# One core, a mixture-of-experts stage: whole experts in order, with an expert's down products behind the next expert's gate and up products

## The chip, the cores and the metric

The kernel runs on one NeuronCore of a Trainium2 chip. The metric is the device time of one launch in microseconds: 894.48 is the median of three runs of the kernel before (893.54 to 895.44). A profile shows one further execution. The core has a matrix engine (PE, its weight loads on a row of their own, PEld), a vector engine (DVE), a scalar engine (ACT), a general engine (POOL) and a queue engine (SP); transfers are issued by SP, ACT and POOL and run on 16 DMA engines.

## The reference

One layer of a streaming encoder over 576 tokens (512 of a prompt, 64 of a sample), all float32: modulation, a normalised projection, two attention mixers, a merge, and then the part that matters here, a mixture of 32 experts:

```
combine = sum(one_hot(expert_id, 32) * w_top)          # two experts of one group per token
for e in range(N_EXPERTS):
    act = silu(n @ w_e_gate[e]) * (n @ w_e_up[e])      # (tokens, 1024) @ (1024, 256), twice
    out = out + combine[:, e] * (act @ w_e_down[e])    # (tokens, 256) @ (256, 1024)
y = y + gate2 * out
```

Each expert has three matrices of 1 MiB: gate, up and down.

## The kernel before

Until about 630 us of the profile the kernel computes everything ahead of the experts, and routes: every expert gets up to 64 slots of tokens. Tokens beyond that go to a loop of overflow blocks at the end, which runs as often as a count read from memory says.

**Rows of tokens.** The normalised rows lie in DRAM (`h2_d`, printed `h_d` by the profile). For two experts at a time `clear_rows` zeroes a tile `xg` of 128 rows on ACT, and `gather_rows` fills it by an indirect DMA on POOL's queue. `turned_rows` turns it into `xT` with 8 transposes on PE (tile `pxg`), and ACT and DVE each copy one half out. The tile `xg` has two buffers.

**One expert** is the generator `expert_parts`, which the program advances step by step: 8 steps of gate and up products into one PSUM tile `gu` (one step per 128 rows of the contraction; the gate product and the up product use two halves of the array), silu and the product `sl`, two small transposes `ta` and their copy `aT`, and the down products `dn`. DVE multiplies `dn` by the row gains `gw` and adds the result to `yr`, rows of the output that `take_rows` has gathered from DRAM. `put_rows` scatters `yr` back. Takes and puts are indirect DMAs on POOL's queue; the rows of an expert are taken two experts ahead.

**Order on PE** (lines 1816 to 1860): the down products of expert e stand inside the gate and up products of expert e+1: three steps of e+1, `ta` of e, two more steps of e+1, `dn` of e, then the last three steps of e+1. After the down products of every even expert stands `turned_rows` for the next two experts, and on POOL, behind the put of that expert, the gather for the two after those.

**Weights.** SP loads the matrices in a fixed order into a ring of 20 buffers (lines 1451 to 1490, `next_tile` counts with `turnstile`): gate, up, down of expert 0, then of expert 1, and so on. Before the first expert starts, 20 matrices have been asked for; from then on each load waits until the matrix that stood in its buffer is used up. At the end of the list the down matrix of expert 30 is held back until the up matrix of expert 31 is on its way (`load_next`). The order on each engine is the order in which the program records it (`manual_schedule`).

## Time and profile before

| | |
|---|---|
| median of three runs | 894.48 us |
| profiled execution, its own time | 895.09 us |
| its span | 893.1 us |
| PE busy | 796.2 us (89%) |
| POOL busy | 289.1 us (32%) |
| read from HBM | 186.86 MB |
| up matrices, from issue to landing | 21.6 us in the middle |
| put of rows, from issue to landing | 6.9 us in the middle |

The profiled execution's time is 2.0 us above its span, and 0.6 us above the median of the runs. In the views below a line names the program line, the engine, the operation and the tiles (out<-in); a figure in brackets is the idle time of the engine just before, and what ended it. [...] DMA share is the mean busy share of the 16 engines.

### The profile page before, as it was taken

How to read it: one execution, taken by the hardware profiler on the slowest of the kernel's cores; microseconds unless marked ns; L12 is line 12 of the kernel's file. 1: busy time of each engine (PE TensorE's matmuls, PEld its weight loads, DVE VectorE, ACT ScalarE, POOL GpSimd, SP SyncE). 2: the span in 40 equal slices, each digit the busy share in tenths (PEclk: the TensorE clock that was granted, in tenths of full speed). 3: DMA queues.
4: the chain of work that ended last, by engine and by line, in shares of the span. 5: the costliest groups of instructions: out<-in, count | busy, mean ns of one | idle time of the engine just before them, and what ended most of it. 6: DMA issues, size and time to landing. Idle time of an engine off the chain costs nothing.

```text
span 893.1 us, 16227 instructions
## 1 busy us (share of the span) xinstructions
PE 796.2 (89%) x6108; PEld 627.2 (70%) x6108; DVE 534.2 (60%) x1285; ACT 310.8 (35%) x754; POOL 289.1 (32%) x380
## 2 busy tenths in 40 slices
PE   6799999999899978999999999985799998878883
PEld 3567897877689967869999999984455554444441
DVE  3458999878956988647052445498355444342441
ACT  4363322475533546557232323432212212111210
POOL 1551432254447740412010103441233343332321
PEclk9899999999999989999999999996799999999997
DMA  9956778321012300126233129989699999999980
GB/s 307 344 168 217 263 242 297 104 62 61 17 61 88 108 4 2 49 97 172 71 95 95 49 97 345 350 301 405 186 415 414 413 412 407 415 413 401 416 333 36
DMA packets 78530, 194.95 MB, mean 218 GB/s; under 512 B 13587, under 2 KB 48387, under 8 KB 66419
## 3 DMA queue, kind: packets, MB, share of 16 engines
q1 hardware_dynamic: 68768, 174.85, 53.6%
q0 software_dynamic: 7424, 14.18, 4.7%
q10 hardware_dynamic: 2258, 4.87, 1.4%
q8 instruction: 49, 0.80, 0.4%
q14 instruction: 31, 0.25, 0.1%
HBM read 186.86 MB, written 18.01 MB: 229 GB/s over the span
## 4 chain that ended last, share of the span: by engine, by line
PE 46%; DMA 24%; DVE 18%; issue 5%; ACT 3%; POOL 2%; SPq 1%; POOLq 0%; DVEq 0%; ACTq 0%
DMA weu<-in_w_e_up 11%; DMA yr<-out_y,sidx 4%; PE pg L410 4%; PE pg L412 4%; PE pg L411 4%; PE gu L1602 3%; PE pj L215 3%; PE pj L217 3%; PE pj L216 3%; DVE K L904 2%; DVE acc L683 2%; DVE m L682 2%; DMA xg<-h_d,gidx 2%; DMA weg<-in_w_e_gate 2%; PE o L799 2%
## 5 line engine op out<-in xcount | busy, mean ns | idle before, releaser
L1602 PE MATMUL gu<-weu,xT 128*64 128x256 f32 x512 | 133.4, 402 | 21.7 <-DMA weu<-in_w_e_up 21.7
L1602 PE MATMUL gu<-weg,xT 128*64 128x256 f32 x512 | 132.2, 398 | 0.5 <-ACT sl L1606 0.5
L215 PE MATMUL pj<-whi,hT 128*128 128x256 f32 (+1 forms) x352 | 107.3, 305 | 0.9 <-DVE yn L472 0.6
L217 PE MATMUL pj<-whi,hT 128*128 128x256 f32 (+1 forms) x352 | 100.7, 286 | 1.3 <-DVE hT L234 1.3
L216 PE MATMUL pj<-wlo,hT 128*128 128x256 f32 (+1 forms) x352 | 100.5, 286 | 0.0
L1602 PEld LDWEIGHTS gu<-weg,xT 128*64 128x64 f32 x512 | 66.6, 141 | 40.8 <-issue 13.3
L203 DVE TENSOR_TENSOR wlo<-raw,whi 128x512 fp32r<-128x512 f32 (+1 forms) x72 | 53.5, 764 | 68.4 <-ACT whi L202 67.8
L1602 PEld LDWEIGHTS gu<-weu,xT 128*64 128x64 f32 x512 | 67.8, 142 | 33.7 <-DMA weu<-in_w_e_up 27.6
L1621 DVE TENSOR_TENSOR gw<-gw,dn 128x512 f32<-128x512 f32 x32 | 22.0, 688 | 105.6 <-PE dn L1619 105.6
L1643 POOL DMA_INDIRECT out_y<-yr,sidx x32 | 33.7, 1053 | 148.2 <-DVE yr L1622 139.2
L410 PE MATMUL pg<-hT,whi 128*128 128x256 f32 (+1 forms) x256 | 78.3, 306 | 0.0
L412 PE MATMUL pg<-hT,whi 128*128 128x256 f32 (+1 forms) x256 | 75.7, 296 | 0.0
L411 PE MATMUL pg<-hT,wlo 128*128 128x256 f32 (+1 forms) x256 | 75.7, 296 | 0.0
L215 PEld LDWEIGHTS pj<-whi,hT 128*128 128x128 f32 x352 | 67.1, 190 | 8.1 <-issue 4.9
L217 PEld LDWEIGHTS pj<-whi,hT 128*128 128x128 f32 x352 | 66.6, 189 | 1.6 <-DVE hT L234 1.5
L216 PEld LDWEIGHTS pj<-wlo,hT 128*128 128x128 f32 x352 | 66.9, 190 | 0.1
L203 POOL TENSOR_TENSOR wlo<-raw,whi 128x512 fp32r<-128x512 f32 (+1 forms) x32 | 41.9, 1332 | 74.2 <-ACT whi L202 54.4
L202 ACT CAST whi<-raw 128x512 fp32r<-128x512 f32 (+1 forms) x104 | 60.3, 624 | 14.8 <-PE pu L1134 14.8
L1619 PE MATMUL dn<-wed,aT 128*64 128x512 f32 x256 | 60.5, 594 | 0.8 <-ACT aT L1614 0.8
L410 PEld LDWEIGHTS pg<-hT,whi 128*128 128x128 f32 x256 | 48.5, 189 | 4.6 <-issue 4.3
L906 POOL TENSOR_TENSOR B<-B,K 128x512 f32<-128x512 f32 (+4 forms) x36 | 35.5, 985 | 41.5 <-DVE K L904 29.2
L411 PEld LDWEIGHTS pg<-hT,wlo 128*128 128x128 f32 x256 | 48.5, 190 | 0.2
(392 smaller groups left out, 2026.4 us busy)
## 6 DMA issues: line engine op xcount, KB each, us to landing
weg<-in_w_e_gate SPq DMA_DIRECT2D x26, 1024.0 KB, 16.5
weu<-in_w_e_up SPq DMA_DIRECT2D x26, 1024.0 KB, 21.6
wed<-in_w_e_down SPq DMA_DIRECT2D x26, 1024.0 KB, 18.5
raw<-in_w_in SPq DMA_DIRECT2D x20, 1024.0 KB, 5.6
wa<-in_w_ada SPq DMA_DIRECT2D x16, 512.0 KB, 10.6
va<-in_w_ada SPq DMA_DIRECT2D x8, 1024.0 KB, 5.3
obT<-in_w_ada SPq DMA_DIRECT2D x8, 1024.0 KB, 6.7
weg<-in_w_e_gate SPq DMA_DIRECT2D x12, 512.0 KB, 11.1
```

The costliest lines, as they stand in the source:

```text
L202: act.copy(hi[:, a:a + 2], raw[:, a:a + 2])
L203: eng.tensor_tensor(lo[:, a:a + 2], raw[:, a:a + 2], hi[:, a:a + 2].bitcast(F32), op=ALU.subtract)
L215: pe.matmul(p[:, :n], a, hi[:, k, :], start=(k == 0), stop=False)
L216: pe.matmul(p[:, :n], a, lo[:, k, :], start=False, stop=False)
L217: pe.matmul(p[:, :n], b, hi[:, k, :], start=False, stop=(k == KD - 1))
L410: pe.matmul(p[:, :b - a], hi[:, k, cs], hT[:, k, a:b], start=(k == 0), stop=False)
L411: pe.matmul(p[:, :b - a], lo[:, k, cs], hT[:, k, a:b], start=False, stop=False)
L412: pe.matmul(p[:, :b - a], hi[:, k, cs], hT[:, k, LP + a:LP + b], start=False, stop=(k == KD - 1))
L906: pool.tensor_tensor(B[:, :nk], B[:, :nk], K[:, 1:nk + 1], op=ALU.mult)
L1602: pe.matmul(gu[64 * j:64 * j + 64, 0:FE], xT[:, k], w[j][k // 4][:, k % 4, :], start=(k == 0), stop=(k == KD - 1))
L1619: pe.matmul(dn[64 * j:64 * j + 64, :], aT[:, k, :], w[2][k][:, 0, j * 512:(j + 1) * 512], start=(k == 0), stop=(k == 1))
L1643: ordered(pool.indirect_dma_start(out=y_rows, out_offset=bass.IndirectOffsetOnAxis(ap=idx_ap, axis=0), in_=yr, in_offset=None, bounds_chec ...
```

## The change

Whole experts follow one another on PE. The generator is split into `expert_up`, `expert_turn` and `expert_down`, and the loop reads: gate and up products of e, after an odd e the turned rows of the next two experts, the down products of e-1, the transposes of e. The list of loads is put in the order of use (`sequence`), and the special case at its end goes. The gather for the experts after next is issued in the iteration of an odd e, behind the put of expert e-1.

```diff
+    sequence = [(0, 0), (0, 1)]
+    for e in range(1, NE):
+        sequence += [(e, 0), (e, 1), (e - 1, 2)]
+    sequence.append((NE - 1, 2))
...
     def next_tile():
-        e, i = divmod(turnstile[0], 3)
+        e, i = sequence[turnstile[0]]
...
+        def down(e):
+            expert_down(aTs.pop(e), ahead.pop(e), gws.pop(e), yrs[e])
+            put_rows(yrs.pop(e), sidx[:, e:e + 1], e)
+
+        gain_rows(0)
+        for e in range(NE):
             j = 64 * (e % 2)
...
-        for e in range(1, NE):
-            begin(e, KD + 1 - 3 - 2)
-            begin(e + 1, 3)
-            begin(e, 1)
-            begin(e + 1, 2 if e < NE - 2 else KD + 1 - 3)
-            begin(e, 9)
-            put_rows(yrs[e], sidx[:, e:e + 1], e)
-            load_next(e)
...
-            if e % 2 == 0:
-                nxt.append(turned_rows(xg, 128))
+            sl = expert_up(xT[:, :, j:j + 64], ahead[e])
+            if e % 2 and e < NE - 1:
+                xT = turned_rows(xg, 128)
                 m = e // 2 + 2
                 if m < NE // 2:
                     xg = clear_rows()
-                    gather_rows(xg, gidx[:, m:m + 1], 128)
-            rows_ahead(e + 2)
+            if e:
+                down(e - 1)
+            gain_rows(e + 1)
+            aTs[e] = expert_turn(sl)
+            for _ in range(2 if e == 0 else 3):
+                if turnstile[0] < len(sequence):
+                    load_tiles(1)
+            if e % 2 and e < NE - 1 and m < NE // 2:
+                gather_rows(xg, gidx[:, m:m + 1], 128)
+            if e + 2 < NE:
+                yrs[e + 2] = take_rows(sidx[:, e + 2:e + 3], e + 2)
...
+        down(NE - 1)
```

On PE, around the turned rows (`pxg`) of experts 4 and 5, it stood like this before; `gu` are products with gate (`weg`) and up (`weu`) matrices, `dn` down products, `ta` the small transposes:

```order
L1612 MATMUL ta<-ident,sl 128x64 x2
L1602 MATMUL gu<-weg,xT 64x256
L1602 MATMUL gu<-weu,xT 64x256
L1602 MATMUL gu<-weg,xT 64x256
L1602 MATMUL gu<-weu,xT 64x256
L1619 MATMUL dn<-wed,aT 64x512 x4
L1582 MATMUL pxg<-ident,xg 128x128 x8
L1602 MATMUL gu<-weg,xT 64x256
```

And it stands like this now:

```order
L1606 MATMUL gu<-weg,xT 64x256
L1606 MATMUL gu<-weu,xT 64x256
L1587 MATMUL pxg<-ident,xg 128x128 x8
L1626 MATMUL dn<-wed,aT 64x512 x4
L1617 MATMUL ta<-ident,sl 128x64 x2
L1606 MATMUL gu<-weg,xT 64x256
```

The turned rows have moved from behind the down products of an even expert to between the last gate and up products of an odd expert and the down products of the expert before it.

On POOL's queue, at the first experts, it stood like this before; `yr` are rows taken, `out_y` rows put, `xg` the gathered rows of two experts, and the numbers tell the tiles apart (7695, 7699, ... belong to experts 0, 1, ...):

```order
L1573 DMA xg_7690<-h2_d_78,gidx_6535 128x1024
L1637 DMA yr_7695<-out_y,sidx_6533 128x512
L1637 DMA yr_7699<-out_y,sidx_6533 128x512
L1643 DMA out_y<-yr_7695,sidx_6533 1152x512
L1573 DMA xg_7763<-h2_d_78,gidx_6535 128x1024
L1637 DMA yr_7768<-out_y,sidx_6533 128x512
L1643 DMA out_y<-yr_7699,sidx_6533 1152x512
```

And now:

```order
L1578 DMA xg_7690<-h2_d_78,gidx_6535 128x1024
L1644 DMA yr_7695<-out_y,sidx_6533 128x512
L1644 DMA yr_7699<-out_y,sidx_6533 128x512
L1644 DMA yr_7740<-out_y,sidx_6533 128x512
L1650 DMA out_y<-yr_7695,sidx_6533 1152x512
L1578 DMA xg_7777<-h2_d_78,gidx_6535 128x1024
L1644 DMA yr_7805<-out_y,sidx_6533 128x512
```

The gather of experts 4 and 5 still stands behind the put of expert 0, but that put now comes after the turned rows of experts 2 and 3 and the gate and up products of expert 1; a third take stands ahead of it.

## Rows read from the trace of the kernel before

**Rows 1.** Windows: start:end, length, busy us of each engine, PEclk, DMA share, GB/s.
```profile
660.00:745.00 85.00, 81.03 (x588) 44.46 (x586) 42.38 (x70) 17.26 (x38) 34.76 (x32) 1.00 1.02 413
745.00:860.00 115.00, 93.89 (x588) 47.66 (x584) 42.56 (x71) 17.50 (x38) 35.66 (x32) 0.94 1.02 411
```
**Rows 2.** Waits of SP's queue, 700 to 860 us: total, times, longest.
```profile
SPq L1488 <- DMA weu<-in_w_e_up: 46.1, 21, 3.4
...
SPq L1488 <- PE gu L1602: 0.4, 2, 0.2
```
**Rows 3.** Timeline of PE: start, duration, line, tiles, [idle before].
```profile
775.42 0.43 PE L1602 MATMUL gu<-weu,xT 128*64 128x256 f32 x1 [1.78 <-DMA weu<-in_w_e_up]
...
820.26 0.43 PE L1602 MATMUL gu<-weu,xT 128*64 128x256 f32 x1 [3.13 <-DMA weu<-in_w_e_up]
...
870.89 0.43 PE L1602 MATMUL gu<-weu,xT 128*64 128x256 f32 x1 [1.02 <-DMA weu<-in_w_e_up]
```
**Rows 4.** Windows of 5 us from the end of each long wait of PE.
```profile
748.90:753.90 5.00, 4.99 (x24) 2.51 (x26) 0.00 (x0) 0.27 (x1) 0.00 (x0) 0.66 1.04 410
775.40:780.40 5.00, 4.98 (x24) 2.53 (x26) 0.00 (x0) 0.27 (x1) 0.26 (x1) 0.66 1.02 415
802.20:807.20 5.00, 4.99 (x32) 2.57 (x33) 0.32 (x1) 0.27 (x1) 0.00 (x0) 1.00 1.02 413
820.30:825.30 5.00, 5.00 (x24) 2.44 (x26) 0.00 (x0) 0.27 (x1) 0.00 (x0) 0.66 1.01 388
838.30:843.30 5.00, 5.00 (x26) 2.55 (x28) 0.00 (x0) 0.27 (x1) 0.00 (x0) 0.72 1.04 417
856.00:861.00 5.00, 4.96 (x32) 2.54 (x33) 0.29 (x1) 0.27 (x1) 0.09 (x1) 1.00 1.03 416
```
**Rows 5.** Chain of waits, 633 to 658 us: start, us, engine or transfer, tile.
```profile
633.68 8.61 DMA xg<-h_d,gidx
...
649.79 1.72 PE dn L1619 x8
651.50 2.59 PE gu L1602 x24
654.09 0.38 PE ta L1612 x2
...
657.20 1.02 PE pxg L1582 x8
```
**Rows 6.** Timeline, the end of expert 0's gate and up products.
```profile
638.10 0.33 SPq L1488 DMA_DIRECT2D wed<-in_w_e_down  x1
...
639.04 0.45 PE L1612 MATMUL ta<-ident,sl 64*128 64x64 f32 x2 [0.96 <-DVE sl L1607]
```
**Rows 7.** Timeline, from down products to a put, and from a put to a gather.
```profile
715.87 1.89 PE L1619 MATMUL dn<-wed,aT 128*64 128x512 f32 x8
...
719.49 1.10 POOL L1643 DMA_INDIRECT out_y<-yr,sidx  x1 [2.45 <-DVE yr L1622]
...
726.33 1.02 POOL L1643 DMA_INDIRECT out_y<-yr,sidx  x1 [4.17 <-PE gu L1602]
727.65 1.02 POOL L1573 DMA_INDIRECT xg<-h_d,gidx  x1 [0.31 <-issue]
```
**Rows 8.** Tile xg: its 16 gathers from issue to landing.
```profile
DMA to landing us min/median/max: 6.0/9.0/9.8
```
**Rows 9.** Timeline, the last two experts.
```profile
874.93 1.89 PE L1619 MATMUL dn<-wed,aT 128*64 128x512 f32 x8
...
876.75 0.45 PE L1612 MATMUL ta<-ident,sl 64*128 64x64 f32 x2
...
877.60 1.94 PE L1619 MATMUL dn<-wed,aT 128*64 128x512 f32 x8 [0.41 <-ACT aT L1614]
...
881.28 1.01 POOL L1643 DMA_INDIRECT out_y<-yr,sidx  x1 [1.71 <-DVE yr L1622]
```

## Prediction

> **What bounds the kernel now.** I read the busy time in windows first, then the waits of SP's queue, the waits of PE, and last the chain of waits through the first experts. From 660 to 860 us the DMA engines show a share of 1.02 at 411 to 413 GB/s without a break, so the weights stream at full rate [rows 1]. PE behaves in two ways under that stream. Up to 745 us it is busy 81.0 of 85 us: it works through the 20 matrices that lie ready at the start, and is itself the slower one. From 745 on it is busy 93.9 of 115 us: it has caught up and waits for the next up matrix [rows 1]. Six of those waits last 1.78 to 3.13 us; the shortest and the longest are shown [rows 3]. SP is not held up by PE: from 700 to 860 us its 21 waits on the landing of up matrices sum to 46.1 us, and its waits on gate and up products to 0.4 us [rows 2]. So buffers are free long before they are needed, and the end is set by the landing of the up matrix of expert 31, at 870.89 us [rows 3]. What follows is a fixed tail of down products, put and closing work.

> Two experts take about 17.8 us of the stream (waits end at 820.3, 838.3 and 856.0, two experts apart [rows 4]). PE needs about 12.3 us for them, as worked out below. The spare 5.5 us is what the change can use up before it costs anything.

> **The weights.** The first 20 loads of the new list are again experts 0 to 5 and the gate and up matrices of expert 6. The next two wait for the gate and up products of expert 0, whose end releases a load at 638.10 now [rows 6]; nothing ahead of that point moves. The last four loads are again gate 31, up 31, down 30, down 31, since the old list already held back down 30. The same bytes in the same ring therefore bring up 31 at the same time; I keep 870.89. This holds while PE gives back buffers faster than the stream fills them, that is below 17.8 us for two experts.

> **The tail.** Now it takes 877.60 - 870.89 = 6.71 us from up 31 to the start of the last down products [rows 3, 9]. After the change the transposes of expert 30 stand before that point. What is left is 16 pairs of products at 2.59 / 12 us each, 3.45, and 0.05 to start; the down products of expert 30, 1.72; and from the last transposes to the last down products 877.60 - 876.75 = 0.85 [rows 5, 9]. That is 6.07, a gain of 0.6 us. The work behind it, put and close, is the same. If PE comes late to that point, the delay is added whole.

> **The gathered rows.** This is the term that decides. In the new order the transposes `pxg` of an odd expert e stand ahead of the down products of e-1, those stand ahead of the put of e-1, the put ahead of the next gather on POOL, and that gather is what `pxg` of e+2 waits for. So there is a loop, once per two experts: `pxg` 1.02 [rows 5], from the start of the down products to the put 719.49 - 715.87 = 3.62, from the put to the gather behind it 727.65 - 726.33 = 1.32 [rows 7], the gather itself 9.0 in the middle [rows 8], and 0.04 to start PE: 15.0 us. PE's own work in the same stretch is two times (3.50 + 1.72 + 0.38) plus 1.02 = 12.2 [rows 5]. So PE would wait some 2.7 us at every `pxg`, 14 times (e = 3 to 29). In the old order the gather had the whole 12.2 us of PE's work between the put and the transposes, and hardly showed. A loop of this kind does not stand in the trace of before, so the gather's landing bounds it: at 6.0 the loop is 12.0 and PE's own work rules; at 9.8 it is 15.8. I take the middle, 9.0, to which nearly all of the 16 gathers lie close.

> When does the loop cost time? Expert 1 can start after the transposes of expert 0, at 639.04 + 0.37 = 639.41 [rows 6], and its products end at 642.9. The gather for experts 2 and 3 has landed at 642.29 [rows 5], so the first `pxg` starts at 642.9. From the last one, at e = 29, PE needs 1.02 + 1.72 + 0.38 + 3.50 + 1.72 + 0.38 = 8.7 us until it is ready for expert 31, so it must start by 870.89 - 8.7 = 862.2. Fourteen rounds may thus take 219.3 us, or 15.66 each. At 15.0 they end at 852.9, and 9.3 us are to spare.

> **The clock.** Those waits have a price of their own. [...] One fall costs (1 - 0.66) x 5 = 1.7 us, or 1.4; over all six waits that is 6.5 / 6 = 1.08 per wait. In the new order the wait ends at `pxg`, and what runs slowly first is `pxg` and the down products, 2.74 us of work that lies inside the loop. So nearly all of the loss lengthens the round, and the next wait is as long as this one. I take 1.0 per round. The bounds are 0 (no fall after waits of 2.7 us) and 1.7 (a fall every time). Fourteen rounds lose 14.0 us: the last `pxg` starts at 852.9 + 14.0 = 866.9, which is 4.7 us late.

> [...]

> **What is hidden.** Row gains for the next expert move on DVE behind the add of e-1; DVE is busy 42.4 of 85 us and has room [rows 1]. The takes now come three experts ahead of their use instead of two, so no add should wait for them. The third take ahead of the first put falls in the pause of the stream before 641 us.

> **Sum.** Tail -0.6, lateness +4.7, together +4.1 us: 899.2 for the profiled execution (895.09), which lies 0.6 above the median of the runs. For the median, 894.48 + 4.1 = 898.6.

> **Rivals.**
> First, the weights still set the end, and it is not slower. If the waits at `pxg` are followed by a lower clock in fewer than 5 or 6 rounds (9.3 us to spare, 1.7 each), or gathers land at 8.5 instead of 9.0 (7 us in 14 rounds), PE is ready when up 31 lands. For it: the gathers late in the trace are no slower than the early ones, and two of six waits cost nothing [rows 4, 8]. The time is 894.48 - 0.6 = 893.9. [...]

> Second, the lower clock follows every wait. Fourteen times 1.6, the mean of the four falls, is 22.4 us: `pxg` of e = 29 at 875.3, 13.1 late, and the time is 894.48 + 13.1 - 0.6 = 907.0. Against it stand the waits before 802.2 and 856.0, which left the clock at 1.00 [rows 4]. [...]

> Third, faster. Up 31 would have to land at least 1.2 us earlier and PE be ready for it. With equal bytes, equal start and an equal end of the list I see only the spread of the stream for it: about 892.

> **How the numbers follow.** The forecast, lateness from 0 to 11 us with its middle at 4.7, gets 0.54; the first rival 0.33; the second 0.08; the third 0.05. Within 0.2% (1.8 us, about what a measurement of this kernel can tell from no change) lie the first rival, except a little of it below, and the part of the forecast with less than 2.4 us of lateness (0.05): 0.37. Slower takes the rest of the forecast and the second rival: 0.57. Faster 0.06. The range goes from 893.2, just under the first rival's time, to 906.5, just under the second's; the forecast's own range is 894.5 to 905.

> **What the profile would show.** Right: PE's waits sit at `pxg` with the gather as releaser, some 14 of 2 to 3 us, starting at e = 3 near 655 us; the time between two `pxg` is about 16 us from 643 to 867; the granted clock falls after most of them; waits on up matrices nearly vanish, and expert 31 starts after 870.9. SP still waits on landings, not on PE, and the DMA share stays at 1.02 to about 860. Wrong: `pxg` finds its rows landed (gathers under 7 us, or a round of 12.5 us); or rounds of 15.5 and less with expert 31 waiting for its up matrix, which is the first rival; or SP waiting on PE, which would break the argument on the stream; or up 31 landing at another time than 869 to 872.

## The result, and the profile after

The changed kernel takes 907.43 us (median of 4 runs, 907.08 to 910.94); the kernel before takes 894.96 beside it (4 runs, 893.54 to 896.62). The ratio is 1.0139, with an interval from 1.0115 to 1.0163: slower by 12.5 us, where 4.1 were forecast and the range ended at 906.5. The profiled execution has a span of 905.8 us and a time of 907.68.

Busy time in windows of the changed kernel, the two that answer to [rows 1] (PE, PEld, DVE, ACT and POOL with instructions, then the granted clock as a share of full speed, the share of the DMA engines, GB/s):

```profile
660.00:745.00 85.00, 72.21 (x477) 37.85 (x477) 34.57 (x56) 15.58 (x32) 26.65 (x25) 0.92 1.01 409
745.00:860.00 115.00, 96.32 (x638) 51.74 (x640) 47.39 (x77) 19.65 (x42) 37.32 (x35) 0.91 1.02 413
```

The transfers are as busy as before, with shares of 1.01 and 1.02. PE is not: in the first window, where it was the slower one and worked at a granted clock of 1.00, it now runs 477 matmuls in 72.2 us at a clock of 0.92 and waits the rest of the time. The waits of PE from 640 to 880 us, and those of SP's queue from 700 to 860, which answer to [rows 2]:

```profile
PE pxg L1587 <- DMA xg<-h_d,gidx: 35.8, 14, 3.4
```

```profile
SPq L1493 <- DMA weu<-in_w_e_up: 41.6, 19, 3.4
SPq L1493 <- DMA wed<-in_w_e_down: 38.7, 19, 3.1
SPq L1493 <- DMA weg<-in_w_e_gate: 38.3, 19, 3.4
...
SPq L1493 <- PE gu L1606: 2.3, 4, 1.6
```

PE's waits on up matrices [rows 3] are gone. In their place stand 14 waits for gathered rows, 35.8 us in sum, all at `pxg`. SP still waits for landings, 118.6 us in the three lines; all its waits on work of PE sum to 3.6 us. The first and the third round of the loop in the timeline, the first at a granted clock of 1.00, the third behind a fall, at 0.50 from 677.10 to 682.10 us (start, us, engine, line, operation, tile; in brackets the wait before it):

```profile
645.13 1.09 PE L1587 MATMUL pxg<-ident,xg 128*128 128x128 f32 x8
...
649.83 1.14 POOL L1650 DMA_INDIRECT out_y<-yr,sidx  x1 [9.31 <-DVE yr L1629]
651.28 1.04 POOL L1578 DMA_INDIRECT xg<-h_d,gidx  x1 [0.31 <-issue]
...
660.97 1.09 PE L1587 MATMUL pxg<-ident,xg 128*128 128x128 f32 x8 [3.20 <-DMA xg<-h_d,gidx]
...
677.06 1.97 PE L1587 MATMUL pxg<-ident,xg 128*128 128x128 f32 x8 [3.44 <-DMA xg<-h_d,gidx]
678.95 3.68 PE L1626 MATMUL dn<-wed,aT 128*64 128x512 f32 x8
...
684.38 1.13 POOL L1650 DMA_INDIRECT out_y<-yr,sidx  x1 [10.48 <-DVE yr L1629]
685.82 1.03 POOL L1578 DMA_INDIRECT xg<-h_d,gidx  x1 [0.31 <-issue]
```

From `pxg` to the put it is 649.83 - 645.13 = 4.70 us at 1.00 and 684.38 - 677.06 = 7.32 behind the fall; from the put to the gather 1.45 (1.32 in [rows 7]); from the gather to the next `pxg` 660.97 - 651.28 = 9.69 here, 8.17 to 9.94 in the 14 rounds with a mean of 9.06. The gathers themselves, which answer to [rows 8], are as before:

```profile
DMA to landing us min/median/max: 5.0/8.9/9.9
```

The last two `pxg`, the down products of expert 28 behind the second, and the last rows, which answer to [rows 9]:

```profile
857.34 1.97 PE L1587 MATMUL pxg<-ident,xg 128*128 128x128 f32 x8 [2.80 <-DMA xg<-h_d,gidx]
...
873.55 1.37 PE L1587 MATMUL pxg<-ident,xg 128*128 128x128 f32 x8 [2.05 <-DMA xg<-h_d,gidx]
874.85 3.30 PE L1626 MATMUL dn<-wed,aT 128*64 128x512 f32 x8
...
890.34 1.94 PE L1626 MATMUL dn<-wed,aT 128*64 128x512 f32 x8 [0.41 <-ACT aT L1619]
```

Fourteen rounds take 873.55 - 645.13 = 228.4 us, 16.32 each, and the last down products start at 890.34 instead of 877.60, 12.7 us later: all of the loss stands before that point. Windows of 5 us behind a `pxg`, as in [rows 4] but with PE's columns alone (PE busy, granted clock, DMA share, GB/s):

```profile
661.00:666.00 5.00, 5.00 (x34) 1.00 1.02 414
677.10:682.10 5.00, 5.00 (x16) 0.50 1.03 415
...
709.40:714.40 5.00, 5.00 (x20) 0.66 1.00 380
740.40:745.40 5.00, 5.00 (x20) 0.66 1.03 421
...
873.60:878.60 5.00, 5.00 (x20) 0.66 0.08 30
```

Behind 10 of the 14 waits the clock is lower, 0.50 to 0.68 over the 5 us, and behind the other four it is 1.00; five of the windows are shown, the last one from the `pxg` of e = 29 on. The wait's length does not tell which: 3.20 us before 660.97 left the clock alone, 1.88 before 709.37 did not.

The start, which answers to [rows 5, 6] (DVE, ACT's queue, ACT, PE and SP's queue, by time):

```profile
628.25 0.19 DVE L1527 TENSOR_TENSOR wslot<-tbw,wslot 128x32 f32<-128x32 f32 x1
...
628.47 0.49 DVE L1598 TENSOR_SCALAR gw<-gate,wslot 128x512 f32<-128x512 f32 x1
...
632.83 0.33 ACTq L1569 DMA_DIRECT2D ov_d<-ovi  x1
...
633.76 0.58 ACT L90 COPY xT<-pxg 128x512 f32<-128x512 f32 x1 [9.20 <-DVE xT L92]
...
634.40 0.69 PE L1606 MATMUL gu<-weg,xT 128*64 128x256 f32 x1 [1.80 <-ACT xT L90]
...
640.21 0.33 SPq L1493 DMA_DIRECT2D weg<-in_w_e_gate  x1
```

The row gains of expert 0 (`gw`, two products of which the first is shown) now run on DVE inside the overflow chain, whose two small stores (`ov_d` and one more) stand on ACT's queue ahead of the evacuation of the first rows. The first release of a buffer is at 640.21, and was at 638.10.

### The profile page after: what moved, and what is told of

Read it like the earlier page. It is cut to its first block, busy times and chain, and to the rows that moved or that the text cites. A ratio compares the mean times of both kernels' runs of the same rounds, so it can differ in the third digit from the quotient of the medians.

```text
span 905.8 us, 16239 instructions
## 1 busy us (share of the span) xinstructions
PE 799.8 (88%) x6108; PEld 630.6 (70%) x6108; DVE 534.6 (59%) x1285; ACT 310.9 (34%) x754; POOL 287.0 (32%) x380
## 4 chain that ended last, share of the span: by engine, by line
PE 38%; issue 21%; DVE 18%; DMA 12%; POOL 6%; ACT 2%; SPq 1%; POOLq 0%; DVEq 0%; ACTq 0%
PE pg L410 4%; DMA out_y<-yr,sidx 4%; PE pg L412 4%; PE pg L411 4%; PE pj L215 3%; POOL yr L1644 3%; PE pj L217 3%; PE pj L216 3%; DVE K L904 2%; DVE acc L683 2%; DVE m L682 2%; POOL out_y L1650 2%; PE o L799 2%; DMA bc<-mod_d 2%; DVE wlo L203 1%
## 5 line engine op out<-in xcount | busy, mean ns | idle before, releaser
L1606 PE MATMUL gu<-weg,xT 128*64 128x256 f32 x512 | 119.5, 387 | 1.8 <-ACT xT L90 1.8
L1606 PE MATMUL gu<-weu,xT 128*64 128x256 f32 x512 | 119.5, 388 | 0.0
L1606 PEld LDWEIGHTS gu<-weg,xT 128*64 128x64 f32 x512 | 68.5, 139 | 37.9 <-ACT xT L90 2.2
L1650 POOL DMA_INDIRECT out_y<-yr,sidx x32 | 36.1, 1129 | 155.9 <-DVE yr L1629 155.9
L1626 PE MATMUL dn<-wed,aT 128*64 128x512 f32 x256 | 74.1, 709 | 0.4 <-ACT aT L1619 0.4
L202 ACT CAST whi<-raw 128x512 fp32r<-128x512 f32 (+1 forms) x104 | 60.3, 624 | 15.3 <-PE pu L1134 14.8
L1587 PE MATMUL pxg<-ident,xg 128*128 128x128 f32 x128 | 22.6, 334 | 38.2 <-DMA xg<-h_d,gidx 38.2
L1610 DVE TENSOR_TENSOR sl<-sl,gu 64x256 f32<-64x256 f32 x32 | 13.6, 424 | 61.2 <-ACT sl L1609 61.2
```

What stands on the lines that cost most here:

```text
L202: act.copy(hi[:, a:a + 2], raw[:, a:a + 2])
L1606: pe.matmul(gu[64 * j:64 * j + 64, 0:FE], xT[:, k], w[j][k // 4][:, k % 4, :], start=(k == 0), stop=(k == KD - 1))
L1626: pe.matmul(dn[64 * j:64 * j + 64, :], aT[:, k, :], w[2][k][:, 0, j * 512:(j + 1) * 512], start=(k == 0), stop=(k == 1))
L1650: ordered(pool.indirect_dma_start(out=y_rows, out_offset=bass.IndirectOffsetOnAxis(ap=idx_ap, axis=0), in_=yr, in_offset=None, bounds_chec ...
```

## The experiments

Each is timed beside the kernel before on the same chip, so the ratios are to be compared; the times of the kernel before differ by up to 2 us between the groups (894.96 to 896.98). Where an expectation says 2.4 or 1.2 GHz it means a granted clock of 1.00 or 0.50: the profile gives the clock as a share of full speed, and no run here shows a rate in GHz.

**The gather ahead of the put.** The loop of the new order is cut in one place:

```diff
                 if m < NE // 2:
                     xg = clear_rows()
+                    gather_rows(xg, gidx[:, m:m + 1], 128)
             if e:
                 down(e - 1)
...
-            if e % 2 and e < NE - 1 and m < NE // 2:
-                gather_rows(xg, gidx[:, m:m + 1], 128)
```

> The order of PE and of the loads stays as in the changed kernel; only the gather for the next two experts is issued earlier, straight behind the clearing of its tile, ahead of the down products of e-1 and of their put on POOL. Theory (the loop through put and gather sets the time): with the put out of the loop a round needs transposes 1.0, evacuation and clearing about 1.5, gather 9.1, some 11.6 us, less than PE's own 12.2 us. The 14 waits at the transposes, 35.8 us in the changed kernel, fall under 8 us in sum, the weights set the end again, and the last down products start near 879 instead of 890.3: 895 to 897 us. Rival (the new order of PE's work or the lower clock by itself sets the time): the rounds stay near 16.3 us and the time stays at 904 to 908. Second rival (the gather is now late behind the clearing): waits of about 1 us stay, and about 900 us.

Measured: 896.4 us, ratio 1.0003 (0.9994 to 1.0012): the whole loss is gone. Its waits of PE, 640 to 880 us, a window as in [rows 1], and a round in its timeline:

```profile
PE gu L1606 <- DMA weu<-in_w_e_up: 20.6, 11, 2.9
...
PE pxg L1587 <- DMA xg<-h_d,gidx: 0.7, 1, 0.7
```

```profile
745.00:860.00 115.00, 93.73 (x582) 49.52 (x583) 42.76 (x70) 17.06 (x37) 34.09 (x32) 0.91 1.02 411
```

```profile
657.22 1.09 PE L1587 MATMUL pxg<-ident,xg 128*128 128x128 f32 x8
...
660.58 1.00 POOL L1578 DMA_INDIRECT xg<-h_d,gidx  x1 [0.30 <-issue]
661.92 1.14 POOL L1650 DMA_INDIRECT out_y<-yr,sidx  x1 [0.35 <-issue]
...
669.94 1.09 PE L1587 MATMUL pxg<-ident,xg 128*128 128x128 f32 x8
```

The gather goes out 3.4 us after `pxg` instead of 6.15, ahead of the put, and a round is 669.94 - 657.22 = 12.7 us, PE's own work. The order of PE's work and that of the loads are those of the changed kernel, so the place of the gather behind the put is a necessary part of the loss. The lower clock alone is not enough for it: from 745 to 860 us PE is granted 0.91 here as in the changed kernel, with its waits now on weights, and nothing is lost.

**Work in the wait, 24 pairs.** In the changed kernel, products that nobody reads go into a spare PSUM bank ahead of each `pxg`; each writes with the weights of the expert just done:

```diff
+    def spin(n, w, xT=None):
+        f = mm_ps("spin")
+        for k in range(n):
+            for j in range(2):
+                pe.matmul(f[64 * j:64 * j + 64, 0:FE], ident[:, 0:64] if xT is None else xT[:, k % KD],
+                          w[j][k % KD // 4][:, k % 4, :], start=(k == 0), stop=(k == n - 1))
...
             if e % 2 and e < NE - 1:
+                spin(12, ahead[e], xT[:, :, j:j + 64])
                 xT = turned_rows(xg, 128)
```

> Changed kernel with 12 more pairs of gate and up products of the odd expert ahead of the transposes, into a spare PSUM bank that nobody reads: 2.6 us of PE work at full clock, placed where PE waits for the gathered rows. Theory (the wait itself costs little beyond the loop; the lower clock behind it lengthens 9 of 14 rounds by 1.7 us): PE keeps 2.4 GHz, every round takes 1.0 + 3.7 + 1.45 + 9.1 = 15.2 us, the transposes at e = 29 start near 858 instead of 873.6, expert 31 waits for its up matrix again, and the time falls to 896 to 898 us although PE has 36 us more to do. Rival (the clock falls for another reason than PE's pause, or the loop alone decides): rounds of 16.3 us or longer and 907 us or more.

Measured: 933.07 us, ratio 1.0418 (1.0403 to 1.0433). The time expected was missed because the edit was twice as large as I had meant: a written product is two instructions in the trace, and the filler takes 5.18 us. Windows of it, with the columns of [rows 1]:

```profile
660.00:745.00 85.00, 85.00 (x680) 50.22 (x678) 32.66 (x54) 13.48 (x29) 24.36 (x23) 1.00 1.01 404
745.00:860.00 115.00, 115.00 (x912) 67.38 (x910) 44.27 (x73) 17.89 (x39) 36.46 (x35) 1.00 1.01 402
```

PE is the bound, with rounds of 17.75 us, and in them it never pauses (85.00 of 85 us and 115.00 of 115) and its clock is 1.00. That is half of the answer.

**Work in the wait, 12 pairs.** The same, half as long.

```diff
             if e % 2 and e < NE - 1:
+                spin(6, ahead[e], xT[:, :, j:j + 64])
                 xT = turned_rows(xg, 128)
```

> As the run with products in the wait, but half as many: each written product is two instructions, so 12 written pairs were 24 pairs and 5.18 us, and PE itself became the bound (rounds of 17.75 us = 12.57 + 5.18, clock 1.00). Now 12 pairs, 2.59 us, so that PE's own round is 12.57 + 2.59 = 15.16 and the loop with gather 15.2. Theory (the lower clock behind the waits is a size of its own): clock 1.00, rounds of 15.2 to 15.5, transposes of e = 29 at 858 to 862, the weights set the end again: 896 to 898 us. Rival (the loop alone is 16.3 us long, whatever the clock): 906 to 908 us, with the waits only shorter by what the products take.

Measured: 895.9 us, ratio 0.9997 (0.9986 to 1.0007). PE has 15 times 2.59 = 39 us more to do than in the changed kernel and yet, by the two ratios (1.0139 and 0.9997), the kernel is 12.7 us faster. Its windows, its waits, a round, and the start of expert 31:

```profile
660.00:745.00 85.00, 83.71 (x640) 47.75 (x638) 36.71 (x60) 16.26 (x34) 27.85 (x27) 1.00 1.02 414
745.00:860.00 115.00, 113.27 (x868) 64.69 (x866) 51.38 (x84) 20.38 (x44) 41.65 (x39) 1.00 1.02 410
```

```profile
PE pxg L1587 <- DMA xg<-h_d,gidx: 3.0, 6, 0.9
```

```profile
756.19 1.09 PE L1587 MATMUL pxg<-ident,xg 128*128 128x128 f32 x8 [0.75 <-DMA xg<-h_d,gidx]
...
760.90 1.14 POOL L1657 DMA_INDIRECT out_y<-yr,sidx  x1 [7.82 <-DVE yr L1636]
762.35 1.03 POOL L1578 DMA_INDIRECT xg<-h_d,gidx  x1 [0.31 <-issue]
...
872.45 0.43 PE L1606 MATMUL gu<-weg,xT 128*64 128x256 f32 x1
```

The loop is still there: `pxg` to put 4.71, put to gather 1.45, and the gather behind it, 15.2 to 16.2 us a round. What is missing is the lower clock (1.00 in both windows, 0.92 and 0.91 in the changed kernel), and with it the loss. So loop and clock are needed together. Part of the expectation was missed: the weights do not set the end here. PE waits for no weight from 640 to 885 us; it starts expert 31 at 872.45, and the last update of the semaphore of up 31 in the trace is at 872.26. PE and the stream arrive level, and a round much longer would have shown in the time.

**Row gains of expert 0 behind the first takes.**

```diff
         yrs = {e: take_rows(sidx[:, e:e + 1], e) for e in range(2)}
+        gw0 = row_gains(wslot[:, 0, 0:1], wslot[:, 1, 0:1])
...
-        gws, aTs = {}, {}
+        gws, aTs = {0: gw0}, {}
-        gain_rows(0)
```

> Changed kernel with one edit: the two products of the row gains of expert 0 are written behind the first takes, in the block before, so that DVE runs them behind the overflow chain again. Theory (they held up ovi, the two small stores on ACT's queue, and behind these the evacuation of the first rows): the gate and up products of expert 0 start at 632.5 instead of 634.4, the first transposes of the loop at 643.1 instead of 645.1, and all that hangs on them, 1.9 to 2.2 us earlier: 905.3 us, since the loop has no slack. Rival (the start is late for another reason, or the loop takes the gain back): expert 0 starts at 634.4, or the time stays at 907.4.

Measured: 908.64 us, ratio 1.0141 (1.0127 to 1.0156): no gain. My theory of the start fell, as far as the time goes. The timeline of its profiled execution:

```profile
626.32 1.48 SPq L1493 DMA_DIRECT2D wed<-in_w_e_down  x2
...
631.14 0.33 ACTq L1569 DMA_DIRECT2D ov_d<-ovi  x1
...
635.70 1.97 PE L1587 MATMUL pxg<-ident,xg 128*128 128x128 f32 x8 [8.30 <-DMA xg<-h_d,gidx]
```

The edit did what it says: the stores go out at 631.14 instead of 632.83. But here the last load before the pause went out at 626.32 (620.36 in the changed kernel), and the first gathered rows were used at 635.70 instead of 630.64. This start differs by several us from profile to profile; the first release lies between 638.10 and 642.09 in these kernels. So only a part of the 2.1 us of the changed kernel's profile can be put down to the row gains. From the second product of the slot weights (`wslot`) to the first store it takes 632.83 - 628.25 = 4.58 us there, and 3.71 both here (631.14 - 627.43) and in the kernel before (630.83 - 627.12): the row gains delay the stores by 0.9 us. Another 1.1 us is that the chain starts later in that profile, at 628.25 instead of 627.12.

**The order of the loads alone**, in the kernel before: the list of the change, and two loads behind expert 0, then three.

> Kernel before with the new order of loads alone (gate and up of e+1 ahead of down of e, two loads behind expert 0 and then three); the order of PE's work is the old one. Theory (the order of the loads is neutral): SP still waits for landings only, the end of the list is the same, and the time is 894.5 within 1 us; some of PE's waits go from the up matrix to the down matrix that now lands behind it. Rival (a down matrix that lands two matrices later holds up PE and with it the release of buffers): 1 to 5 us slower, with SP waiting on products of PE.

Measured: 898.18 us, ratio 1.0019 (1.0008 to 1.0029), 1.7 us slower: nearer to neutral than to the loss, but not neutral. Two rows of its timeline:

```profile
649.20 0.33 SPq L1493 DMA_DIRECT2D wed<-in_w_e_down  x1
...
872.44 0.43 PE L1607 MATMUL gu<-weu,xT 128*64 128x256 f32 x1 [1.98 <-DMA weu<-in_w_e_up]
```

The third load after the pause goes out at 649.20, since it takes the place of a matrix of expert 1; up 31 lands at 872.44, 1.55 us later than in [rows 3]. SP's waits on work of PE between 700 and 860 us sum to 1.2 us, so the rival's mechanism is not seen.

**The shift from expert 1 on**, to test that restart: the early gather, with down products and put of expert 0 ahead of expert 1 and its down matrix third in the list.

```diff
-    sequence = [(0, 0), (0, 1)]
-    for e in range(1, NE):
+    sequence = [(0, 0), (0, 1), (0, 2), (1, 0), (1, 1)]
+    for e in range(2, NE):
...
+            if e == 0:
+                down(0)
-            for _ in range(2 if e == 0 else 3):
+            for _ in range(2 if e == 1 else 3):
```

> The run with the early gather, and the shift of the down products begins one expert later: down products and put of expert 0 stand behind its own transposes, ahead of expert 1, as in the kernel before, and its down matrix is again the third of the list (loads 3, 2, 3, 3). Theory (the new order of the loads delays the restart of the stream: the third load after the pause took the place of a matrix of expert 1, and went out at 643.97 and 649.20 us in the runs with the early gather and with the load order alone, against 641.82 in the kernel before): the third load goes out near 642 again, up 31 lands 1.3 us earlier than in the run with the early gather (872.24), near 871, and the time falls by as much, ratio to the kernel before 0.998 to 0.9995. Rival (the restart is made up for later, since the queue is held by landings alone): third load at 642 but up 31 still near 872 and ratio 1.000.

Measured: 898.83 us, ratio 1.0021 (1.0008 to 1.0034): no gain over the early gather alone, whose interval (0.9994 to 1.0012) it overlaps. Two of its rows:

```profile
642.23 0.45 SPq L1493 DMA_DIRECT2D wed<-in_w_e_down  x1
...
872.08 0.63 PE L1606 MATMUL gu<-weu,xT 128*64 128x256 f32 x1 [1.96 <-DMA weu<-in_w_e_up]
```

The third load goes out at 642.23 as intended, and up 31 lands no earlier. So the third load is not what delays up 31; what does, and whether this kernel is slower than the early gather, stays open.

**The overflow chain behind the takes**, with the early gather and the row gains moved, so that nothing stands ahead of the first evacuation.

```diff
-        overflow_blocks()
         xT = turned_rows(xg, 128)
...
         yrs = {e: take_rows(sidx[:, e:e + 1], e) for e in range(2)}
+        overflow_blocks()
```

> Changed kernel with three edits: the early gather of the first run; the row gains of expert 0 behind the first takes; and the whole overflow chain with its two stores on ACT's queue behind these takes too, so that nothing stands ahead of the evacuation of the first rows. Theory: the evacuation on ACT starts 1.2 us after the first transposes (in the run with the early gather alone 633.15 - 629.91 = 3.24 us), the first products of expert 0 and the first release of a buffer come up to 2.0 us earlier, and since the weights set the end, so does the end: 0.5 to 2 us below the kernel before, ratio 0.998 to 0.9995. Rival (the landing of the first gathered rows sets the start, and varies by more): ratio 1.000 within 0.001, first release between 638 and 640 as in the other runs.

Measured: 898.36 us, ratio 1.0025 (1.0011 to 1.0039): slower. POOL, DVE and PE in its timeline:

```profile
638.40 0.24 POOL L1560 IOTA rq<- 128x32 f32 x1
...
640.89 0.42 DVE L1610 TENSOR_TENSOR sl<-sl,gu 64x256 f32<-64x256 f32 x1
...
641.37 0.50 PE L1617 MATMUL ta<-ident,sl 64*128 64x64 f32 x2 [3.48 <-DVE sl L1610]
```

The chain has an iota on POOL, which now stands behind a gather and takes; DVE waits for it with the gating product of expert 0 queued behind, and the row gains, moved too, stand between them on DVE (639.42 to 640.85). PE waits 3.48 us instead of 0.96. I had looked at two queues and moved the work past a third.

**Products at the start, and at both ends.** The kernel just told, with 20 pairs that nobody reads where PE waits ahead of expert 0:

```diff
+        spin(4, ahead[0])
         weight_table()
+        spin(4, ahead[0])
         xT = turned_rows(xg, 128)
+        spin(2, ahead[0])
```

> The kernel with the three edits, and products that nobody uses on PE while it waits ahead of expert 0: 8 pairs ahead of the weight table, 8 behind it, 4 behind the first transposes. [...] Theory: PE is at 2.4 GHz there, the first buffer comes free 2 us earlier, and the end with it: ratio to the kernel before 0.995 to 0.997, near 893 us. Rival (the added products delay the transposes or the weight table, or the clock stays down): no gain over the kernel without them, or 1 to 2 us slower.

Measured: 897.76 us, ratio 1.0030 (1.0016 to 1.0044): no gain over the kernel without them that the intervals can tell. The clock rose as intended, to 1.00 from 631.90 to 641.00 us, where the kernel before has 0.66 over the products of expert 0 (632.54 to 638.10), but the first release came at 638.83, no earlier than the 638.40 of the kernel without these products, and the wait at expert 0's transposes is still 3.22 us. Then the kernel with the later shift, and 8 such pairs ahead of each of the experts 28 to 31:

```diff
         for e in range(NE):
             j = 64 * (e % 2)
+            if e >= NE - 4:
+                spin(4, ahead[e - 1])
             sl = expert_up(xT[:, :, j:j + 64], ahead[e])
```

> The kernel with the later shift and only the products ahead of experts 28 to 31 (8 pairs, 1.73 us each). Theory: PE is at 2.4 GHz when up 31 lands, the last down products start 6.1 to 6.4 us after that instead of 7.85, and the time is 1.4 to 1.8 us below the run with the later shift. Rival (the tail is not at the lower clock in most executions): as the run with the later shift, within 0.5 us, or later by what the products take.

Measured: 897.4 us, ratio 1.0005 (0.9996 to 1.0015), 1.4 us below the run with the later shift, as expected, though the intervals of the two ratios still touch. The first up product of expert 31 and the last down products in its timeline:

```profile
872.98 0.43 PE L1606 MATMUL gu<-weu,xT 128*64 128x256 f32 x1
...
879.16 1.94 PE L1633 MATMUL dn<-wed,aT 128*64 128x512 f32 x8 [0.41 <-ACT aT L1626]
```

From the one to the other it is 6.2 us, against 879.94 - 872.08 = 7.9 in the run with the later shift, and the granted clock is 1.00 from 870 to 882 us where that run has 0.54 and 0.60 from 872 to 876: the tail runs at 1.00 as the theory says. In these two profiles the end is only 0.8 us earlier, as up 31 comes 0.9 us later. And the same with the products at the start and the row gains moved, the overflow chain left in its place:

```diff
+        spin(4, ahead[0])
         weight_table()
         overflow_blocks()
+        spin(4, ahead[0])
         xT = turned_rows(xg, 128)
+        spin(2, ahead[0])
...
+        gw0 = row_gains(wslot[:, 0, 0:1], wslot[:, 1, 0:1])
```

> The kernel with the later shift, the row gains of expert 0 behind the first takes, and products that nobody uses where PE waits: 8 pairs ahead of the weight table, 8 ahead of the first transposes, 4 behind them, and 8 (1.73 us) ahead of each of the experts 28 to 31. Theory: expert 0 runs at 2.4 GHz and gives its first buffer back up to 2 us earlier, which moves the stream and with it the end; and the last wait on up 31 no longer leaves PE at 1.2 GHz in the tail (7.85 us from up 31 to the last down products in the run with the early gather, 6.07 worked out at full clock): ratio 0.995 to 0.998, 892 to 894 us. Rival (the first release hangs on the landing of the first gathered rows, and added products only delay it): 1.000 to 1.002.

Measured: 895.83 us, ratio 0.9987 (0.9975 to 0.9999). It has the lowest ratio here, 1.2 us below the kernel before, and the interval ends just under 1; the 0.995 to 0.998 that I expected were missed. The tail gives about 1.4 us by the run above. The other 1.6 against the run with the later shift are not seen in its profile, whose first release is at 642.00, later than in all runs but one and not earlier as in the theory; where they come from stays open.

## Why the prediction was wrong

The direction and the mechanism were right: the waits sit at `pxg` with the gather as releaser, 14 of them, from e = 3 on; up matrices are no longer waited for; the clock falls behind most waits; SP waits for landings. The profile showed each of these as foretold, and the run with the gather ahead of the put and the one with 12 pairs in the wait confirm loop and clock separately. What failed is the step from the rounds to the lateness. The last `pxg`, forecast at 866.9 and 4.7 us late, started at 873.55, 11.3 us behind the 862.2 that it had to meet, and the tail behind it was longer than forecast too. At the start of the last down products that is 12.74 - 4.1 = 8.6 us, in four terms that all err on the same side (8.7 with their rounding).

**The gathered rows**, 2.9 us. The loop was 15.0; without the lower clock it measures 4.70 + 1.45 + 9.06 = 15.2, and 14 rounds make 2.9. The put takes 1.13 us, where I had taken a put row of 1.02 [rows 7], though another row of that group has 1.10.

**The clock in the rounds**, 1.6 us. I took 1.0 per round, 14.0, from the windows of [rows 4]: 0.66 to 0.72 with 24 to 26 matmuls in four, 1.00 with 32 in two. Nine of the 14 rounds have a longer way from `pxg` to the put (6.22 to 7.32 instead of 4.70), 15.6 us in sum. The mean of a fall, 1.73, was the upper bound that I had given; the share of falls is close to four of six.

**The tail**, 2.0 us. From `pxg` of e = 29 to the last down products I had 8.7 + 6.07 = 14.8; it is 890.34 - 873.55 = 16.8. The wait before that `pxg` has a fall behind it too (0.66 in the last window, 3.30 us for down products that take 1.89 at 881.96, where the clock is 1.00). I had counted a lower clock in 14 rounds. The first of them has no wait ahead of it, and the last wait has no round behind it, only the tail: from that `pxg` to its put it is 6.34 instead of 4.70, so 1.6 us are the fall's. The other 0.4 are mostly three down products, which take 1.82 to 1.87 us of PE to the next work where I had taken 1.72 [rows 5].

**Nothing ahead of that point moves**, 2.2 us, was false: the first `pxg` of the loop is at 645.13, not 642.9. Row gains of expert 0 that I had called hidden on DVE moved into a chain that ACT's queue waits for. Of the 2.2 us 0.9 are theirs by the traces and 1.1 a chain that starts later in this profile; moving them back gave nothing in the time, with a profile in which the first gathered rows came later.

The second rival, the lower clock after every wait, gave 907.0 and is nearest to the time, but not by its reason: four waits left the clock alone, and start, loop and tail make up for them. The first rival's premise, no loss without the falls, is borne out by the run with 12 pairs: at a granted clock of 1.00 the loop costs no time that the interval can tell, though PE and not the weights came last there. The waits here last 1.67 to 3.44 us, and the clock fell behind 10 of the 14, not behind every one.

The spare time of 9.3 us was compared with one term at a time. Without any fall the rounds would have ended at 645.13 + 14 x 15.2 = 857.9, ahead of 862.2; with the falls they end 11.3 us behind it. Every us beyond a threshold counts in full, so the small terms had to be added up on its far side, together; I had added them one rival at a time.

Of the weights the prediction held that the new list brings up 31 at the same time. In the changed kernel nothing waits for it, but the trace has the last update of its semaphore at 869.89 us, against 870.85 in the kernel before (0.04 us ahead of the product that waits for it there). So it landed 1.0 us earlier, within the 869 to 872 that the prediction named, and has no part in this result. In the run with the new list alone up 31 lands 1.55 us later and the time is 1.7 us longer; why the same list gives both is open.

## What to carry to other kernels

When an order is changed so that a fetch is issued behind a result of the same round, write the loop down and move the fetch ahead of that result: here it had only to go out ahead of one put on its queue, and the loss was gone. Behind 10 of the 14 waits of PE here, 1.67 to 3.44 us long, the clock was lower, and nine of these falls made the way from `pxg` to the put 1.73 us longer in the mean: price such waits with the slower work behind them, up to and including the last one before the end. Before work is called hidden, look at every queue that its neighbours stand on, in both directions.
